# Two MLP matrices as seven block products in place of eight, in a two-layer streaming encoder step

## The chip, the core and the metric

The kernel runs on one core of one Trainium2 chip. The metric is the device time of one execution in microseconds (us), taken as the median of several runs. The engines are TensorE (PE in the profile; PEld is its weight load), VectorE (DVE), ScalarE (ACT), GpSimd (POOL) and SyncE (SP), which issues transfers.

## The reference

Two layers work on 1056 tokens (1024 of a prompt, 32 of a running sample) of width 1024. Layer 0 mixes tokens by forgetting attention, layer 1 by a gated linear recurrence; each is followed by a squared-ReLU MLP with a hidden width of 4096. Everything is float32.

```python
def rmsnorm(x, g):
    xf = x.astype(jnp.float32)
    y = xf * lax.rsqrt(jnp.mean(xf * xf, axis=-1, keepdims=True) + EPS)
    return (y * g.astype(jnp.float32)).astype(x.dtype)
...
        x = x + rmsnorm(out, post_mix_norm[layer])
        h = rmsnorm(x, pre_ffn_norm[layer])
        u = jax.nn.relu(h @ ffn_w_up[layer])
        x = x + rmsnorm((u * u) @ ffn_w_down[layer], post_ffn_norm[layer])
```

`out` is the mixer's output times W_out. The change rewrites the part from W_out to the last line, once per layer.

## The kernel before, in words

Activations lie with features on partitions and tokens along the free axis, in three chunks of C = 352 tokens. Every product is taken in float32r: a matrix is split exactly into a high and a low part, and `mm3` (L152) adds three passes, high by high, low by high, high by low, in one PSUM bank. A weight unit of 128 x 1024 comes in by DMA (`wr`); `load_w` (L122) casts the high part `wh` on ACT (L142) or POOL (L144), by turns, and DVE subtracts it to get the low part `wl` (L145).

`tail` (L436) is called once per layer. Its stages:

- Output projection (`po`), chunk by chunk, with all eight weight units loaded once. ACT copies each result out of PSUM, squares it, and POOL adds up the squares (L194). `postnorm` (L271) scales the chunk (L279, DVE) and adds the residual (POOL and DVE by turns, L162 and L284); `prenorm` (L222) splits the next product's input into `hh` and `hl` (ACT L226, DVE L231, POOL L162). The factor of the second norm, `prestat` (L236), is put on after the products, so the products don't wait for it.
- The MLP, two hidden tiles at a time. `up_one` (L491) takes 24 matmuls of 352 columns per hidden tile and chunk; ACT takes relu (L499) and the square's high part (L501), POOL squares again (L162), DVE subtracts (`ul`, L503). `down_one` (L510) takes, per two hidden tiles, 6 matmuls for each of eight output tiles and each chunk, and DVE adds the bank to the running sum `ya` (L520).
- The last two groups go chunk by chunk, so that `finish` (norms, and the next layer's input, or the output `y`) of one chunk lies beside the products of the next. In layer 1 the last chunk is normed with tokens on partitions (`end_open` L328, `end` L345).

One loop of the MLP holds 144 matmuls of `up` and 144 of `dn`; both layers together hold 4608 + 4608 of 352 columns.

The order in which an engine's instructions stand is set by the scheduler of the tile framework from the program's order; what stands in `with self.soon()` goes ahead of other work. Each engine works through its own list in order, so an instruction that waits holds back all behind it.

## Time and profile before

| | us |
|---|---|
| median of 3 runs | 3001.73 |
| lowest, highest | 2998.78, 3002.98 |
| profiled execution's span | 2996.0 |
| median less span | 5.7 |
| PE busy | 2942.2 (98%) |
| DVE busy | 1734.0 (58%) |
| ACT busy | 934.1 (31%) |
| POOL busy | 967.0 (32%) |
| mean granted TensorE clock | 0.997 of 2.4 GHz |

The span runs from the first to the last instruction; the median also holds what lies around it. PE's matmuls overlap in its pipeline, so the time of one is read from the distance between two starts, not from its own duration. Shares of busy time are means over stages: what holds a stage up is read from that stage's own window. Names such as `dn` and `ya` are the program's tiles, and L158 is a line of the kernel.

### The profile page before, as it was taken

The numbers are of one execution on the slowest core, as the hardware profiler recorded it, in microseconds if no ns is written. First come the engines' busy times: TensorE is split into PE (matmuls) and PEld (weight loads), VectorE is DVE, ScalarE is ACT, GpSimd is POOL, SyncE is SP. The second block draws the span as 40 slices with busy tenths as digits, with TensorE's granted clock in tenths as the row PEclk, the third lists the DMA queues.
The fourth block names the chain that finished last, engine by engine and source line by source line (L and its number), as shares of the span: only waits on it lengthen the run. The fifth ranks groups of instructions, "written<-read, shape, count | busy, mean of one in ns | idle before, by whom it ended". The sixth has DMA issues, their size and how long they took to land.

```text
span 2996.0 us, 46448 instructions
## 1 busy us (share of the span) xinstructions
PE 2942.2 (98%) x18511; PEld 2855.2 (95%) x18511; DVE 1734.0 (58%) x2980; ACT 934.1 (31%) x1915; POOL 967.0 (32%) x1151
## 2 busy tenths in 40 slices
...
GB/s 152 62 52 44 48 53 48 51 112 147 106 74 57 43 43 50 36 57 49 37 82 95 35 59 41 47 27 120 140 118 76 36 57 43 43 50 36 57 61 69
DMA packets 217817, 195.59 MB, mean 65 GB/s; under 512 B 14312, under 2 KB 193648, under 8 KB 217472
## 3 DMA queue, kind: packets, MB, share of 16 engines
q1 hardware_dynamic: 216576, 192.49, 21.5%
q8 instruction: 145, 2.38, 0.3%
...
q0 software_dynamic: 1024, 0.13, 0.0%
...
## 4 chain that ended last, share of the span: by engine, by line
PE 89%; DVE 5%; issue 1%; POOL 1%; ACT 1%; DMA 1%; SPq 0%; DVEq 0%; POOLq 0%; ACTq 0%
PE up L158 24%; PE dn L158 24%; PE hj L158 8%; PE pj L158 8%; PE gp L158 6%; PE po L158 5%; PE lv L1166 1%; PE ss L753 1%; PE pv L880 1%; PE pv L879 1%; PE pv L878 1%; PE st L867 1%; PE st L866 1%; PE mp L835 1%; PE lv L1181 1%
## 5 line engine op out<-in xcount | busy, mean ns | idle before, releaser
L520 DVE TENSOR_TENSOR ya<-dn,ya 128x352 f32<-128x352 f32 x672 | 348.3, 522 | 550.4 <-PE dn L158 550.4
L162 POOL TENSOR_TENSOR rl<-rl 128x352 f32<-128x352 f32 x192 | 190.2, 999 | 1031.7 <-ACT uh L501 1029.3
L145 DVE TENSOR_TENSOR wl<-wr,wh 128x1024 fp32r<-128x1024 f32 x203 | 280.4, 1382 | 147.0 <-ACT wh L142 84.6
L158 PE MATMUL dn<-uh,wl 128*128 128x352 f32 x1440 | 356.9, 323 | 0.0
L158 PE MATMUL dn<-uh,wh 128*128 128x352 f32 x1440 | 353.7, 324 | 2.5 <-DVE ya L520 2.5
L158 PE MATMUL dn<-ul,wh 128*128 128x352 f32 x1440 | 353.5, 323 | 0.0
L499 ACT ACTIVATE rl<-up 128x352 f32<-128x352 f32 x192 | 88.8, 463 | 783.1 <-PE up L158 712.8
L158 PE MATMUL up<-hh,wl 128*128 128x352 f32 x1536 | 291.5, 323 | 0.0
L158 PE MATMUL up<-hh,wh 128*128 128x352 f32 x1536 | 287.5, 323 | 2.1 <-ACT wh L142 1.7
L158 PE MATMUL up<-hl,wh 128*128 128x352 f32 x1536 | 288.1, 323 | 0.0
L158 PEld LDWEIGHTS up<-hh,wh 128*128 128x128 f32 x1536 | 253.5, 188 | 3.1 <-ACT wh L142 2.3
L158 PEld LDWEIGHTS dn<-uh,wh 128*128 128x128 f32 x1440 | 251.3, 188 | 4.4 <-DVE ya L520 4.4
L158 PEld LDWEIGHTS up<-hh,wl 128*128 128x128 f32 x1536 | 254.4, 188 | 0.0
L158 PEld LDWEIGHTS up<-hl,wh 128*128 128x128 f32 x1536 | 254.1, 188 | 0.0
L158 PEld LDWEIGHTS dn<-uh,wl 128*128 128x128 f32 x1440 | 252.6, 188 | 0.0
L158 PEld LDWEIGHTS dn<-ul,wh 128*128 128x128 f32 x1440 | 251.8, 188 | 0.0
L144 POOL TENSOR_SCALAR wh<-wr 128x1024 fp32r<-128x1024 f32 x109 | 120.8, 1108 | 294.3 <-PE pj L158 93.0
L503 DVE TENSOR_TENSOR ul<-rl,uh 128x352 fp32r<-128x352 f32 x192 | 142.6, 754 | 124.9 <-POOL rl L162 124.8
L142 ACT CAST wh<-wr 128x1024 fp32r<-128x1024 f32 x94 | 98.7, 1050 | 347.2 <-PE up L158 221.5
L876 DVE TENSOR_TENSOR pl<-pf,ph 128x512 fp32r<-128x512 f32 x192 | 124.5, 652 | 59.9 <-POOL ph L875 34.7
L875 POOL TENSOR_SCALAR ph<-pf 128x512 fp32r<-128x512 f32 x192 | 125.2, 654 | 51.6 <-PE pv L879 24.7
L869 ACT ACTIVATE pf<-st,ncol 128x512 f32<-128x512 f32 x192 | 109.7, 578 | 71.2 <-PE st L867 40.1
...
## 6 DMA issues: line engine op xcount, KB each, us to landing
wr<-in_ffn_w_up_dram SPq DMA_DIRECT2D x64, 512.0 KB, 4.0
wr<-in_ffn_w_down_dram SPq DMA_DIRECT2D x64, 512.0 KB, 3.8
wr<-in_fox_w_in_dram SPq DMA_DIRECT2D x32, 512.0 KB, 4.1
wr<-in_hgrn_w_in_dram SPq DMA_DIRECT2D x32, 512.0 KB, 4.1
...
```

Of the source, the lines that this page charges most:

```text
L142: self.s.copy(wh, raw)
L144: self.g.tensor_scalar(out=wh, in0=raw, scalar1=1.0, scalar2=0.0, op0=ALU.mult, op1=ALU.add)
L145: self.v.tensor_tensor(wl, raw, wh.bitcast(F32), op=ALU.subtract)
L158: self.nc.tensor.matmul(ps, lhsT=ws[kk][a], rhs=xs[kk][b], start=i == 0, stop=i == tot - 1)
L162: self.g.tensor_tensor(out, a, b, op=op)
L499: self.s.activation(rl, ps[:, :C], AF.Relu)
L503: self.v.tensor_tensor(ul, rl, uh.bitcast(F32), op=ALU.subtract)
L520: self.v.tensor_tensor(ys[n][:, o], ps[:, :C], ys[n][:, o], op=ALU.add)
L753: nc.tensor.matmul(ss[:, :C], lhsT=self.blk, rhs=sq, start=True, stop=True)
L869: self.s.activation(pf[:, :N], ps[:, :N], AF.Exp, bias=self.ncol[:, b, head:head + 1])
L875: self.g.tensor_scalar(out=ph[:, :N], in0=pf[:, :N], scalar1=1.0, scalar2=0.0, op0=ALU.mult, op1=ALU.add)
L876: self.v.tensor_tensor(pl[:, :N], pf[:, :N], ph[:, :N].bitcast(F32), op=ALU.subtract)
```

## The change

Tokens are taken in four quarters of G = 264; group c holds quarters c and c + 2, which play the two column blocks of the input. A unit is 256 rows by 256 columns of output by input features at a time, four pairs of feature tiles long: its four 128 x 128 blocks (`a11` to `a22`) and the two token quarters give seven products in place of eight, in the order 1, 5, 2, 6, 3, 7, 4 (`unit`). A product is 3 passes of 4 matmuls of 264 columns, so a unit has 84 matmuls per group and 168 for both.

- Weight side of a unit: 1 MB by DMA, four sums of blocks on POOL (`form`, 512 columns each), seven casts on ACT and seven subtracts on DVE (`cut`, 512 columns each), into a ring of three.
- Input side: seven forms of each pair of tiles, 7 x 264 columns, split in high and low (`forms`, `t_forms`, `split`).
- `up`: the results are put together by ACT copies, DVE adds from PSUM and a POOL add; relu and square are one DVE operation on each of four blocks; four POOL subtracts make the next product's forms, which go to memory (`uf`). The first NA = 4 units run for group 0 alone and again for group 1 alone, their weights loaded and formed twice; twelve run for both groups.
- `down`: step s takes the four pairs s - 3 to s for output block (s + 1) mod 4. `get_forms` brings a pair's forms back from memory and splits them. Steps 0 to 13 take both groups; 14 to 18 first group 0, then group 1, with group 0's `finish` ahead of group 1's step 15.
- The output projection goes by groups (`project`), with W_out loaded twice. The norm's factor is applied ahead of the product, as rows; the special form of the last chunk is gone. In the recurrence's projections ACT takes the results out of PSUM and no factor is multiplied on; chunks there are quarters.

In both layers together 10752 matmuls of 264 columns stand in place of 9216 of 352. The diff, cut to what is spoken of:

```diff
-TOK0 = (0, 128, C - 128)
+G = NT // 4
...
+LAG = 14
+NA = 4
+EV = 6
...
+    def forms(self, c, x, r, kind, layer, scratch, place):
+        for kp in range(4):
+            f = scratch(kp)
+            for j, o in ((2 * kp, f[:, 0:8:7]), (2 * kp + 1, f[:, 2:5:2])):
+                self.v.scalar_tensor_tensor(out=o, in0=x[:, j], scalar=self.gcol(kind, layer, j), in1=r,
+                                            op0=ALU.mult, op1=ALU.mult)
+            self.t_forms(f, (self.g, self.v, self.g, self.v))
+            self.F[c].append(place(kp))
+            self.split(self.F[c][kp], f[:, 0:7], 0, 7)
+    def t_forms(self, f, engs):
+        for e, o, a, b in zip(engs, (1, 5, 3, 6), (7, 4, 4, 2), (0, 7, 1, 3)):
+            e.tensor_tensor(f[:, o], f[:, a], f[:, b], op=ALU.subtract)
+    def split(self, F, src, a, b):
+        lo, hi = F[:, 0, a:b], F[:, 1, a:b]
+        self.s.copy(hi, src)
+        self.v.tensor_tensor(lo, src, hi.bitcast(F32), op=ALU.subtract)
+    def unit(self, cs, raw, pairs, evac):
+        nk = len(pairs)
+        w = raw.rearrange("p (k e) (m q) -> p k e m q", e=2, m=2)
...
+        def form(i, a, b=None, op=None):
+            self.ns += 1
+            t = self.S[:, self.ns % 3, :, 0:nk]
+            src = a
+            if b is not None:
+                self.nx += 1
+                src = self.Sx[:, self.nx % 2, 0:nk]
+                self.g.tensor_tensor(src, a, b, op=op)
+            S[i] = (t[:, 0], t[:, 1], src)
+        def cut(i):
+            lo, hi, src = S[i]
+            self.s.copy(hi, src)
+            self.v.tensor_tensor(lo, src, hi.bitcast(F32), op=ALU.subtract)
+        add, sub = ALU.add, ALU.subtract
+        ps = {}
+        for f, p in enumerate((1, 5, 2, 6, 3, 7, 4)):
+            if p == 1:
+                form(1, a11)
+            elif p == 5:
+                form(5, a21, a22, add)
+                form(2, a12)
+                form(6, S[5][2], a11, sub)
+            elif p == 6:
+                form(3, a12, S[6][2], sub)
+            elif p == 3:
+                form(7, a11, a21, sub)
+            elif p == 7:
+                form(4, a22)
+            cut(p)
+            lo, hi, _ = S[p]
+            fresh = p in (1, 5, 2, 4)
+            bank = {1: "X", 6: "X", 7: "X", 5: "Z", 3: "Z", 2: "Y", 4: "V"}[p]
+            for c in cs:
...
+                n, tot = 0, 3 * nk
+                for a, b in ((hi, 1), (lo, 1), (hi, 0)):
+                    for i, kp in enumerate(pairs):
+                        self.nc.tensor.matmul(o, lhsT=a[:, i], rhs=F[kp % 4][:, b, f], start=fresh and n == 0,
+                                              stop=n == tot - 1, skip_group_check=not fresh)
+                        n += 1
+                with self.soon():
+                    evac(p, c, o)
...
+    def tail(self, w_out, layer, sc=None):
...
+                def project(c):
+                    for o in range(NJ):
+                        wh, wl = self.load_w(self.col_unit(w_out, o * 128))
+                        for h in range(2):
...
+                        acc = self.sq_add(0, ys[c][:, o], o)
+                    return acc
+                acc = project(0)
+                acc2 = self.postnorm(0, ys[0], xa, acc, 1, layer, sc and sc(0))
+                self.put_x(0, xa)
+                scr = [ob.tile([128, 8, G], F32, name=f"fs{layer}_{i}") for i in range(2)]
+                self.forms(0, xa, self.factor(acc2), 2, layer, lambda kp: scr[kp % 2], lambda kp: form_tile(fa))
+                ys.append(pair(new(self.rh if last else ob, "yb", 16)))
+                acc = project(1)
+                xb = pair(new(self.rh, "xb", 16))
+                acc2 = self.postnorm(1, ys[1], xb, acc, 1, layer, sc and sc(1))
+                self.put_x(1, xb)
...
+            def up(i, cs, sts):
+                raw = load(wu[:, i * 256:i * 256 + 256].rearrange("(k p) m -> p k m", p=128))
...
+                def act(eng, c, slot, z):
+                    eng.scalar_tensor_tensor(out=st[c][:, slot], in0=z, scalar=0.0, in1=z, op0=ALU.max, op1=ALU.mult)
+                def evac(p, c, o):
...
+                        if p == 4:
+                            z = T[5, c]
+                            self.gtt(z, z, t, ALU.add)
+                            act(self.v, c, 4, z)
+                        self.v.tensor_tensor(t, o, t, op=ALU.add)
+                        act(self.v, c, {2: 0, 3: 7, 4: 2}[p], t)
+                    if p == 4:
+                        self.t_forms(st[c], (self.g, self.g, self.g, self.g))
+                        nc.sync.dma_start(self.uf[i][c], st[c][:, 0:7])
+                self.unit(cs, raw, range(4), evac)
+            for i in range(NA):
+                if i == 3:
+                    s = ust
+                else:
+                    s = fb.tile([128, 8, G], F32, name=f"us{layer}_{i}", tag=f"f{3 - i % 2}")
+                up(i, (0,), (s,))
+            with self.soon():
+                self.forms(1, xb, self.factor(acc2), 2, layer, lambda kp: fscr,
+                           lambda kp: form_tile(fb, tag=f"f{kp}"))
+            hst = [new(self.rh, "hs", 8) for i in range(4)]
+            for i in range(NA):
+                up(i, (1,), (hst[i % 4],))
+            for i in range(NA, 16):
+                up(i, (0, 1), (hst[2 * (i % 2)], hst[2 * (i % 2) + 1]))
+            Y = [pair(new(self.rh, "Y", 16)) for c in range(2)]
+            def get_forms(p, c, land):
+                for i, (a, b) in enumerate(((0, 2), (2, 4), (4, 6), (6, 7))):
+                    self.nl += 1
+                    t = land[:, 2 * (self.nl % 4):2 * (self.nl % 4) + b - a]
+                    nc.sync.dma_start(t, self.uf[p][c][:, a:b])
+                    self.split(self.F[c][p % 4], t, a, b)
+            def down(s, cs, load):
+                m = (s + 1) % 4
+                pairs = range(max(0, s - 3), min(s, 15) + 1)
+                first, final = s < 4, s > 14
+                r = pairs[0] * 256
+                raw = load(wd[r:r + 256 * len(pairs), m * 256:m * 256 + 256].rearrange("(k p) m -> p k m", p=128))
+                T = {}
...
+                def evac(p, c, o):
+                    y = lambda a, b: Y[c][:, 2 * m + a, b]
+                    if p in (5, 6, 7):
+                        t = T[p, c] = ev("e")
+                        self.s.copy(t, o)
+                    if p == 1 and first:
+                        self.s.copy(y(0, 0), o)
+                    elif p in (1, 2):
+                        self.v.tensor_tensor(y(0, 0), o, y(0, 0), op=ALU.add)
+                    elif p == 7:
+                        w = T[5, c]
+                        if not first:
+                            self.gtt(w, w, y(1, 1), ALU.add)
+                        self.gtt(y(1, 1), w, t, ALU.add)
+                    elif p in (3, 4):
+                        t, d = (T[6, c], y(0, 1)) if p == 3 else (T[7, c], y(1, 0))
+                        if not first:
+                            self.gtt(t, t, d, ALU.add)
+                        self.v.tensor_tensor(d, o, t, op=ALU.add)
+                        squares(c, 0 if p == 3 else 1)
+                self.unit(cs, raw, pairs, evac)
+            self.acc, self.nsq, self.nl = [None, None], [0, 0], 0
+            for s in range(LAG):
+                for c in range(2):
+                    get_forms(s, c, st)
+                down(s, (0, 1), load)
+            get_forms(LAG, 1, st)
+            for s in range(LAG, 19):
+                if s < 16:
+                    get_forms(s, 0, st)
+                down(s, (0,), load)
...
+            def finish(c):
+                acc = self.postnorm(c, Y[c], xs[c], self.acc[c], 3, layer, more=not last)
...
+                for j in range(NJ):
+                    y = xs[c][:, j]
+                    self.v.scalar_tensor_tensor(out=y, in0=y, scalar=self.gcol(0, layer + 1, j), in1=r,
+                                                op0=ALU.mult, op1=ALU.mult)
+                    self.s.copy(hh[:, j], y)
+                    (self.g if j % 3 == 2 else self.v).tensor_tensor(hl[:, j], y, hh[:, j].bitcast(F32), op=ALU.subtract)
+            self.h = [None, None]
+            for s in range(LAG, 19):
+                if s == 15:
+                    finish(0)
+                    get_forms(s, 1, st)
+                down(s, (1,), load if s < 15 else load2)
+            finish(1)
```

How the order moves, at three places. DVE at the start of layer 0's MLP: `rw` is the norm's factor per token, `yo`, `x` and `hl` the last chunk's norm and split, `ul` the MLP's own subtract. Before:

```order
L279 SCALAR_TENSOR_TENSOR yo_9250<-yo_9250,gain,rw_9497 128x352 x8
L503 TENSOR_TENSOR ul_9622<-rl_9682,uh_9621 128x352
L284 TENSOR_TENSOR x_0_9482<-x_0_9482,yo_9250 128x352 x2
L284 TENSOR_TENSOR x_1_9483<-x_1_9483,yo_9250 128x352
L231 SCALAR_TENSOR_TENSOR hl_9548<-x_0_9482,gain,hh_9547 128x352
L284 TENSOR_TENSOR x_1_9483<-x_1_9483,yo_9250 128x352
L231 SCALAR_TENSOR_TENSOR hl_9548<-x_1_9483,gain,hh_9547 128x352
L231 SCALAR_TENSOR_TENSOR hl_9548<-x_0_9482,gain,hh_9547 128x352
L241 TENSOR_TENSOR yo_9250<-yo_9250 128x352
L231 SCALAR_TENSOR_TENSOR hl_9548<-x_0_9482,gain,hh_9547 128x352
L503 TENSOR_TENSOR ul_9624<-rl_9712,uh_9623 128x352
```

and now, where `fs` is the scratch of group 1's input forms, `F` their split, `Y`/`e`/`hs` the evacuation of group 1's first unit and `S` the cuts of weights:

```order
L260 SCALAR_TENSOR_TENSOR fs_938_10034<-xb_932_9976,gain,rr_10555 128x2x264 x2
L270 TENSOR_TENSOR fs_938_10034<-fs_938_10034 128x264 x2
L276 TENSOR_TENSOR F_981_10596<-fs_938_10034,F_981_10596 128x1848
L260 SCALAR_TENSOR_TENSOR fs_938_10034<-xb_932_9976,gain,rr_10555 128x2x264 x2
L270 TENSOR_TENSOR fs_938_10034<-fs_938_10034 128x264 x2
L276 TENSOR_TENSOR F_982_10605<-fs_938_10034,F_982_10605 128x1848
L530 TENSOR_TENSOR e_10628<-Y_10651,e_10628 128x264
L518 SCALAR_TENSOR_TENSOR hs_983_10608<-e_10628 128x264
L301 TENSOR_TENSOR S_10038<-Sx_10039,S_10038 128x512 x2
```

Before, subtracts of the running product stand between the pieces of the norm. Now the forms of group 1 stand in one block, of which the last rows are shown (the same three kinds come four times), behind the last unit of group 0 and ahead of group 1's first.

DVE at the end of layer 0: the norm of a finished chunk or group. Before, with `dn` the products of the next chunk:

```order
L279 SCALAR_TENSOR_TENSOR ya_9898<-ya_9898,gain,rw_15960 128x352 x8
L284 TENSOR_TENSOR x_0_15942<-x_0_15942,ya_9898 128x352 x2
L520 TENSOR_TENSOR ya_9899<-dn_16067,ya_9899 128x352
L284 TENSOR_TENSOR x_1_15943<-x_1_15943,ya_9898 128x352
L231 SCALAR_TENSOR_TENSOR hl_16015<-x_0_15942,gain,hh_16014 128x352
L284 TENSOR_TENSOR x_1_15943<-x_1_15943,ya_9898 128x352
L520 TENSOR_TENSOR ya_9899<-dn_16084,ya_9899 128x352
L231 SCALAR_TENSOR_TENSOR hl_16015<-x_0_15942,gain,hh_16014 128x352
L520 TENSOR_TENSOR ya_9899<-dn_16101,ya_9899 128x352
L241 TENSOR_TENSOR ya_9898<-ya_9898 128x352
L231 SCALAR_TENSOR_TENSOR hl_16015<-x_1_15943,gain,hh_16014 128x352
```

and now, `Y_1211` being group 0's sum, `xs` the residual, `Y_1212` group 1's sum and `S` the cuts of weights of group 1's step 15:

```order
L241 SCALAR_TENSOR_TENSOR Y_1211_13968<-Y_1211_13968,gain,rr_17809 128x528 x8
L243 TENSOR_TENSOR xs_1444_17682<-xs_1444_17682,Y_1211_13968 128x528 x4
L232 TENSOR_TENSOR st_8900<-st_8900 128x528 x2
L276 TENSOR_TENSOR F_982_10605<-st_8900,F_982_10605 128x528 x2
...
L634 SCALAR_TENSOR_TENSOR xs_1444_17682<-xs_1444_17682,gain,rr_17859 128x528 x8
L585 TENSOR_TENSOR Y_1212_13969<-X_17917,Y_1212_13969 128x264
L301 TENSOR_TENSOR S_10038<-Sx_10039,S_10038 128x512
L637 TENSOR_TENSOR h_1466_17877<-xs_1444_17682,h_1465_17876 128x528
L301 TENSOR_TENSOR S_10038<-Sx_10039,S_10038 128x512
```

Before, the adds that empty PSUM stand between the norm's rows from the third on. Now the scaling, the adds and the next layer's scaling of group 0 stand ahead of the first cut of group 1's step.

POOL in the steady part of the first product. Before, squares of `rl` and casts of weights:

```order
L144 TENSOR_SCALAR wh_11808<-wr_11806 128x1024
L162 TENSOR_TENSOR rl_11597<-rl_11597 128x352
L162 TENSOR_TENSOR rl_11847<-rl_11847 128x352
L162 TENSOR_TENSOR rl_11877<-rl_11877 128x352
L144 TENSOR_SCALAR wh_12196<-wr_12194 128x1024
L162 TENSOR_TENSOR rl_11907<-rl_11907 128x352
```

and now, where `Sx` are sums of weight blocks, `hs` the forms of the result and `e` evacuated products:

```order
L295 TENSOR_TENSOR Sx_10039<-raw_940_10036 128x512
L295 TENSOR_TENSOR Sx_10039<-raw_941_10037 128x512
L295 TENSOR_TENSOR Sx_10039<-Sx_10039,raw_941_10037 128x512
L270 TENSOR_TENSOR hs_985_10610<-hs_985_10610 128x264
L270 TENSOR_TENSOR hs_986_10611<-hs_986_10611 128x264
L186 TENSOR_TENSOR e_12833<-e_12833,e_12958 128x264
L270 TENSOR_TENSOR hs_985_10610<-hs_985_10610 128x264 x2
L186 TENSOR_TENSOR e_12848<-e_12848,e_12972 128x264
L295 TENSOR_TENSOR Sx_10039<-raw_941_10037,Sx_10039 128x512
```

Before, one operation of 352 columns per 24 matmuls and a cast now and then. Now sums of 512 and of 264 columns follow one another, all of them two tensors from SBUF.

## Rows read from the trace of the kernel before

**Rows 1.** The page's span, and part 1: busy time of each engine.

```profile
span 2996.0 us, 46448 instructions
PE 2942.2 (98%) x18511; PEld 2855.2 (95%) x18511; DVE 1734.0 (58%) x2980; ACT 934.1 (31%) x1915; POOL 967.0 (32%) x1151
```

**Rows 2.** Part 4 of the page: the chain's share by line.

```profile
PE up L158 24%; PE dn L158 24%; PE hj L158 8%; PE pj L158 8%; PE gp L158 6%; PE po L158 5%; PE lv L1166 1%; PE ss L753 1%; PE pv L880 1%; PE pv L879 1%; PE pv L878 1%; PE st L867 1%; PE st L866 1%; PE mp L835 1%; PE lv L1181 1%
```

**Rows 3.** The chain in order of time (start us, us, what), MLP of layer 0.

```profile
956.07 7.76 PE up L158 x48
1002.46 7.76 PE up L158 x48
```

**Rows 4.** Windows: length, busy us (x count) per engine, PE clock, DMA share, GB/s.

```profile
728.00:917.50 189.50, 186.93 (x1173) 185.15 (x1172) 90.79 (x130) 78.45 (x171) 75.43 (x73) 1.00 0.31 102
917.50:1493.50 576.00, 576.00 (x3579) 576.00 (x3579) 267.47 (x423) 92.39 (x171) 101.63 (x98) 1.00 0.16 46
1493.50:1640.00 146.50, 131.28 (x795) 126.85 (x795) 103.55 (x170) 55.85 (x118) 74.22 (x77) 0.97 0.28 88
```

**Rows 5.** Timeline of PE at 167 us: start us, us, operation, columns.

```profile
167.44 0.28 PE L866 MATMUL st<-QA,KA 128*128 128x256 f32 x1
167.55 0.28 PE L867 MATMUL st<-QX,KB 97*128 97x256 f32 x1
167.68 0.32 PE L158 MATMUL pj<-hl,wh 128*128 128x352 f32 x1
...
168.40 0.23 PE L866 MATMUL st<-QA,KA 128*128 128x128 f32 x1
168.46 0.28 PE L867 MATMUL st<-QX,KB 97*128 97x128 f32 x1
```

**Rows 6.** Three lines' instructions: ns min/median/max, first and last start.

```profile
L503 DVE TENSOR_TENSOR ul<-rl,uh x192: 506/525/1409, 823.8 to 2944.1; 128x352 fp32r<-128x352 f32 x192
L520 DVE TENSOR_TENSOR ya<-dn,ya x672: 507/524/527, 910.7 to 2982.6; 128x352 f32<-128x352 f32 x168
L194 POOL TENSOR_TENSOR sa<-sa,sj x72: 928/947/1807, 730.8 to 2981.3; 128x352 f32<-128x352 f32 x72
```

**Rows 7.** Timelines of DVE, then of POOL, at 2214 us.

```profile
2214.40 1.26 DVE L241 TENSOR_TENSOR yo<-yo 128x352 f32<-128x352 f32 x1
2215.59 3.64 DVE L231 SCALAR_TENSOR_TENSOR hl<-x,gain,hh 128x352 fp32r<-128x352 f32 x3
...
2214.08 1.20 POOL L194 TENSOR_TENSOR sa<-sa,sj 128x352 f32<-128x352 f32 x1
2215.25 1.22 POOL L162 TENSOR_TENSOR hl<-yo,hh 128x352 fp32r<-128x352 f32 x1
2216.43 1.23 POOL L241 TENSOR_TENSOR yo<-yo 128x352 f32<-128x352 f32 x1
2217.62 1.22 POOL L194 TENSOR_TENSOR sa<-sa,sj 128x352 f32<-128x352 f32 x1
```

**Rows 8.** Parts 5 (busy us, mean ns) and 6 (KB, us to landing) of the page.

```profile
L144 POOL TENSOR_SCALAR wh<-wr 128x1024 fp32r<-128x1024 f32 x109 | 120.8, 1108 | 294.3 <-PE pj L158 93.0
L142 ACT CAST wh<-wr 128x1024 fp32r<-128x1024 f32 x94 | 98.7, 1050 | 347.2 <-PE up L158 221.5
wr<-in_ffn_w_up_dram SPq DMA_DIRECT2D x64, 512.0 KB, 4.0
```

**Rows 9.** Timeline of PE: the last two matmuls of `dn`.

```profile
2981.91 0.48 PE L158 MATMUL dn<-ul,hh 128*128 128x352 f32 x2
```

**Rows 10.** Timeline of PE behind a stop at 1581 us.

```profile
1586.49 4.24 PE L158 MATMUL hj<-hh,wh 128*128 128x352 f32 x16 [4.91 <-ACT sj L191]
1590.57 1.46 PE L158 MATMUL hj<-hh,wl 128*128 128x352 f32 x8
```

587 lines of the change are left out of this document (225 added, 362 removed).

## The prediction

> **What bounds the kernel now.** I read the page's engine shares first: TensorE (PE) is busy 98% of a span of 2996.0 us, VectorE (DVE) 58%, ScalarE (ACT) 31%, GpSimd (POOL) 32% [rows 1]. The chain that ended last says the same by line: `up` and `dn`, the two MLP products, hold 24% each [rows 2]. In order of time the chain shows the MLP's beat: a run of 48 `up` matmuls begins every 46.39 us [rows 3]. Two hidden tiles by three chunks of 24 matmuls, and eight output tiles by three chunks of 6, are 288 matmuls, so one of 352 columns takes 46.39 / 288 = 0.161 us. The windows show what fills the beat: in 576.0 us PE is never idle, while DVE works 267 us and POOL 102 [rows 4]. Around the MLP it is otherwise: between 1493.5 and 1640 us, where one layer's last norms run into the next projection, PE is busy 131 of 146.5 us [rows 4]. So the MLP is bound by matmuls, and its edges by elementwise work. The change must be weighed at both.
>
> **What it removes.** Per layer 16 + 16 units of 168 matmuls of 264 columns replace 4608 of 352. In both layers 9216 become 10752. A matmul's time follows its columns: neighbours of 256 start 0.11 to 0.13 us apart, one of 128 is followed after 0.06, 352 need 0.161 [rows 3, 5]. I take 264 / 352 of 0.161 = 0.1208 us (0.116 would be the low end from 256 columns, 0.1214 the high one from a line through 128 and 352). 9216 x 0.161 = 1484 and 10752 x 0.1208 = 1299 us: **186 us less**, an eighth (179 to 237 by the ends). A unit for both groups then lasts 168 x 0.1208 = 20.3 us, for one group 10.1.
>
> **What it adds: two engines that must take turns.** Block sums, splits and forms are elementwise with both inputs in SBUF. What such work costs beside POOL is in the trace. DVE's `ul` subtract (two SBUF inputs) takes 525 ns in the middle and up to 1409; its `ya` add on the same 352 columns, with one input from PSUM, never leaves 507 to 527; POOL's `sa` add takes 947 and up to 1807 [rows 6]. The stretch at 2214 us shows why: DVE and POOL step together, POOL starting every 1.18 us where it needs 0.947 alone, each DVE operation stretched to 1.2 [rows 6, 7]. A pair of 352 columns costs both engines 1.19 us. I split this as 525 to 947: 1.21 ns a column for DVE's two-SBUF work, 2.17 for POOL's, to be added where both are loaded. DVE's PSUM operations and ACT stay out of the sum. The Trainium skill, "SBUF — State Buffer", section "SBUF: two separate sides", calls the shared port pair an exclusive lock for the whole instruction. By that, full durations would add, 1.47 us a pair; the row has 1.19, so the measurement is used and the rule becomes a rival below.
>
> *Per unit.* The weight side is four POOL sums and seven DVE subtracts of 512 columns (seven ACT casts of 512 beside them, at 1050 ns for 1024 [rows 8] at most 7.4 us, hidden). Up, per group: four DVE activations, and five POOL sums of 264. Down, per group: 1848 columns of DVE split and four POOL sums of 264.
> - Up, both groups: 5696 x 1.21 + 4688 x 2.17 = 17.1 us of taking turns, under 20.3 of PE: hidden.
> - Down, both: 7280 x 1.21 + 4160 x 2.17 = 17.8: hidden, with 2.5 us to spare.
> - Up, one group: 4640 x 1.21 + 3368 x 2.17 = 12.9, **over** 10.1 of PE. The weight side doesn't shrink when one group uses it.
>
> *Norm and forms of one group.* DVE: scaling 8 x 528, adds 4 x 528, squares 2 x 528, gains 16 x 264, forms 8 x 264, splits 4 x 1848, factors 8 x 264: 23232 columns. POOL: adds 4 x 528, squares 5 x 528, forms 8 x 264: 6864. 28.1 + 14.9 = 43 us. Before, the like of it for a chunk lay beside other chunks' products: from 728 to 917.5 us PE was idle only 2.6 us [rows 4].
>
> **Where this lands on the path,** place by place, the work that takes turns against PE's:
> - Out projection of group 1 (384 matmuls, 46.4 us) beside group 0's norm and forms: 43, plus eight `wl` subtracts of 1024 (9.9), four POOL casts at 1108 ns [rows 8] (4.4) and squares (7.0) = 64. Loss 18 a layer.
> - The four units for group 0 alone (40.6) beside group 1's norm and forms. In DVE's order the forms stand behind the last unit's cuts and ahead of group 1's first; so PE waits for them: 4 x 12.9 + 43 = 95, loss 54.
> - The same four units again for group 1: 51.6 against 40.6, loss 11.
> - Steps 14 to 18 for group 0 alone: the pairs run out (4, 4, 3, 2, 1), so 294 matmuls, 35.5 us. DVE: 3.5 x 3584 of cuts, two pairs' splits, squares: 17296 columns; POOL: 3.5 x 2048 of sums, 20 x 264, squares: 15088. 53.7, loss 18.
> - The same for group 1, with group 0's finish in DVE's and POOL's queues ahead of step 15's cuts: in layer 0 14784 and 5808 columns more (30.5), in layer 1, without squares, forms and splits, 6336 and 2112 (12.2). 84 and 66 against 35.5: loss 49 and 30.
> - Group 1's finish: in layer 0 30.5 against 144 matmuls of the next projection that group 0 allows (17.4), loss 13; in layer 1 nothing is left, loss about 21.
>
> Twice 18 + 54 + 11 + 18 is 202, and 49 + 30 + 13 + 21 is 113: 315 us. Given back are the old stalls: 3 and 18 us (146.5 less 795 x 0.161) [rows 4] and 14 behind the last `dn` at 2982 [rows 9], together 35. 315 - 35 - 186 = **+94 us**.
>
> **Edits with one answer.** The inner forms go to memory and back, 1.9 MB a unit, written in one stage and read in the other, beside 1 MB of weights: 2.9 MB in 20.3 us, some 140 GB/s in a stage that now moves 46 at a DMA share of 0.16 [rows 4], so half the queues' time, and a whole step ahead; nothing. W_out loaded twice: its DMA lands in 4 us like other weights [rows 8], the casts are counted. The hgrn evacuation on ACT and 264-column chunks move the same columns; nothing, within 10 us either way. Restarts: after 4.91 us of idle, 16 matmuls took 4.1 us for 2.6 [rows 10], so 1.5 us a stop and under 20 for all places; I leave it in the range, since stalls made of many short waits need not cost it. The Trainium skill, "TensorE: Matmul & The Clock Gate", section "Back-to-back issue gap", has columns / 2.4 + 2.5 ns for an isolated matmul; by that 264 would take 112.5 and the sum fall by 89 us, to +5. For 352 it gives 149 where the beat has 161, so it is not used.
>
> The sum is against the profiled execution: 2996.0 + 5.7 around the span is the median of 3001.7. Forecast: **3096 us**, slower by 3.1%.
>
> **Rivals.**
> - *The two engines rarely meet* (faster). Where POOL's and DVE's operations fall into each other's gaps, or wait for ACT anyway, each place costs only its busier engine at undisturbed durations, 1.49 ns a DVE column and 2.69 of POOL. Then the out projection costs nothing (46), group 0's four units 67 - 41 = 26, group 1's nothing, group 0's ends 5 (POOL 40.6 against 35.5), group 1's 21 and 11, the finishes 5 and 18. 2 x (26 + 5) + 55 = 117; 117 - 35 - 186 = -104, **2898 us**. For it: most `ul` subtracts are undisturbed [rows 6]. Against: these are the places where both queues are full, as at 2214 us [rows 7]. It decides if the pair costs less than about 0.9 us.
> - *The steady units slip too* (much slower). 17.1 to 17.8 of 20.3 us leaves 12 to 16%, with in-order queues, three buffers for cut weights (two products, 5.8 us, ahead) and two for sums. If each of the 52 two-group units slips by 1.5 us, 78 more: **3174 us**. For it: DVE carries PSUM adds on top, six to eight a unit. Against: before, DVE had the same sort of mixture at 46% and PE never waited [rows 4].
> - *The lock holds for the whole instruction.* With 1.49 and 2.69 ns added, up takes 21.1 and down 22.0 us per unit, so 34 us a layer are lost in the steady part alone; group 0's four units lose 76, the projection 32, group 1's units 23, the ends 31, then 68 and 46, 20 and 25: 551 in all, 330 over before, **3332 us**. Against it: rows 7 beside rows 6, 1.19 and not 1.47. By the Trainium skill's rule that is quoted above from "SBUF — State Buffer" it would go so.
> - *Matmuls of 264 don't get shorter in proportion.* At 0.1214, +6 us; part of the range.
>
> **How the numbers follow.** Forecast 0.47, with 3040 to 3150 of its own; engines rarely meet 0.25; steady units slip 0.18; whole-instruction lock 0.07; what I don't see 0.03. No change means within 0.2%, 6 us, about what a measurement of this kernel can tell. The first rival is all below that, the others above; the unseen is shared out: faster 0.26, same 0.02, slower 0.72. The range, 2885 to 3210, leaves out the whole-instruction lock and the outer third of the fast case.
>
> **What would show it.** In the changed profile: `Y`, `X`, `Z`, `V` matmuls 0.121 us apart and a two-group unit in 20.3 us with PE busy throughout; PE with holes, and a granted clock below full after them, in the four-unit stages, the single-group steps and around the finishes, DVE and POOL full there; the split subtracts of 528 stretched well over 0.78 us where POOL works. The forecast is wrong if PE stays full in the four-unit stage (then the engines do not take turns there), or if the two-group units last 21.5 us or more.

## The result and the profile after

The changed kernel takes **3227.8 us** (median of 4, 3224.5 to 3229.4) against 3001.1 for the kernel before: ratio 1.0756, 95% interval 1.0741 to 1.0771, **7.6% slower**. The sign was as forecast, the size was not: +227 us where the sum gave +94, and outside the range of 2885 to 3210.

The page after; span and busy time of each engine [rows 1], then the chain's shares [rows 2]:

```profile
span 3226.6 us, 55945 instructions
PE 2885.5 (89%) x21197; PEld 2747.2 (85%) x21197; DVE 2287.1 (71%) x3589; ACT 1374.5 (43%) x2904; POOL 1747.8 (54%) x1801
PE 70%; DVE 15%; issue 5%; POOL 3%; ACT 3%; DMA 3%; SPq 0%; DVEq 0%; POOLq 0%; ACTq 0%
```

PE was busy 98% and is now busy 89%; DVE holds 15% of the chain. In order of time, the chain in the steady part of layer 0's first product is the counterpart of [rows 3]: the seven products of a two-group unit, 24 matmuls each, and the first of the next unit.

```profile
1010.19 2.92 PE X L333 x24
1013.10 2.95 PE Z L333 x24
1016.05 2.91 PE Y L333 x24
1018.96 2.94 PE X L333 x24
1021.90 2.92 PE Z L333 x24
1024.82 2.93 PE X L333 x24
1027.76 2.92 PE V L333 x24
1030.68 2.91 PE X L333 x24
```

A unit lasts 1030.68 - 1010.19 = 20.49 us, 0.122 us a matmul where the sum had 0.1208: the product side was right within 1%. The windows of after, in the columns of [rows 4], show where the time went. In order: four units of group 0; group 1's first unit; its other three; the twelve two-group units; steps 0 to 2 of the second product; steps 3 to 13; steps 14 to 18 of group 0; the same of group 1; the start of the next layer's projection; then, of layer 1, the four units of group 0, the last steps of group 1 and the tail.

```profile
850.60:936.20 85.60, 55.31 (x341) 51.27 (x341) 77.11 (x91) 30.05 (x59) 64.31 (x49) 0.78 0.40 130
936.20:971.60 35.40, 15.26 (x88) 13.49 (x87) 22.34 (x25) 9.73 (x13) 11.71 (x11) 0.64 0.00 0
971.60:1010.40 38.80, 35.02 (x254) 32.94 (x254) 35.89 (x44) 16.33 (x34) 32.77 (x27) 0.96 0.48 162
1010.40:1256.40 246.00, 246.00 (x2019) 246.00 (x2018) 168.12 (x258) 87.31 (x189) 173.45 (x168) 1.00 0.40 145
1256.40:1303.90 47.50, 37.78 (x254) 34.56 (x253) 39.91 (x70) 27.64 (x70) 22.33 (x25) 0.86 0.69 219
1303.90:1528.90 225.00, 225.00 (x1850) 225.00 (x1850) 170.55 (x247) 106.99 (x231) 140.35 (x124) 1.00 0.47 142
1528.90:1580.00 51.10, 43.44 (x295) 38.81 (x294) 43.98 (x61) 25.62 (x60) 41.33 (x42) 0.96 0.43 139
1580.00:1676.40 96.40, 53.52 (x302) 46.23 (x300) 78.55 (x104) 40.54 (x87) 66.55 (x58) 0.77 0.26 80
1676.40:1760.00 83.60, 44.61 (x314) 42.69 (x315) 49.36 (x56) 28.10 (x53) 35.48 (x32) 0.74 0.22 67
2363.80:2467.80 104.00, 60.06 (x345) 53.70 (x345) 97.67 (x114) 37.22 (x70) 71.76 (x54) 0.73 0.35 118
3109.30:3191.60 82.30, 59.00 (x346) 49.02 (x344) 63.11 (x88) 32.57 (x73) 56.09 (x51) 0.83 0.23 75
3191.60:3226.60 35.00, 11.91 (x52) 7.43 (x52) 19.98 (x26) 6.18 (x12) 8.68 (x7) 0.60 0.19 62
```

PE is never idle in the fourth and sixth rows (DVE is busy 68 and 76% there, POOL 71 and 62%); everywhere else it has holes, and in the first row DVE is busy 77 of 85.6 us. So the rival in which the steady units slip did not happen, nor the one in which a whole instruction locks the other engine out. The Trainium skill, "SBUF — State Buffer", section "SBUF: two separate sides", has the shared port pair as an exclusive lock for the whole instruction. By that rule the rival put a two-group unit at 21.1 to 22.0 us, and the chain above has 20.49. The margin is smaller than it looks: with the undisturbed durations of `e10` below (DVE 692 ns for 512 columns, 708 for 528, 434 for 264) and those of POOL's sums beside an idle DVE in the changed kernel (1288 ns for 512, 750 for 264), the rival's sum is about 21 us for both kinds of unit, by my estimate.

The elementwise groups that replace those of [rows 6], from part 5 of the page:

```profile
L301 DVE TENSOR_TENSOR S<-Sx,S 128x512 fp32r<-128x512 f32 (+3 forms) x352 | 305.1, 871 | 105.8 <-ACT S L300 105.0
L295 POOL TENSOR_TENSOR Sx<-raw 128x512 f32<-128x512 f32 (+3 forms) x176 | 234.6, 1335 | 167.4 <-DVE S L301 162.9
L270 POOL TENSOR_TENSOR hs<-hs 128x264 f32<-128x264 f32 x224 | 221.6, 1004 | 93.0 <-DVE hs L518 91.3
```

Two holes have names of their own. PE's timeline (start, length, line; in brackets the idle time before and what ended it) in layer 0, in group 1's step 15 and at the start of the next layer's projection:

```profile
1623.46 2.13 PE L205 MATMUL cs<-st,ones 128*128 128x264 f32 x4 [25.14 <-DVE st L232]
...
1713.00 2.13 PE L205 MATMUL cs<-st,ones 128*128 128x264 f32 x4 [25.71 <-DVE st L232]
1726.76 3.54 PE L182 MATMUL hj<-h,wh 128*128 128x264 f32 x16 [11.64 <-ACT wh L166]
```

`cs` are a norm's squares, summed over partitions by a matmul with ones. They stand in PE's list ahead of products that don't depend on them, and wait for the squares that `finish` sums up late. DVE's timeline in the first of these holes:

```profile
1603.42 8.64 DVE L241 SCALAR_TENSOR_TENSOR Y<-Y,gain,rr 128x528 f32<-128x528 f32 x8
1611.99 5.86 DVE L243 TENSOR_TENSOR xs<-xs,Y 128x528 f32<-128x528 f32 x4
1617.77 0.69 DVE L232 TENSOR_TENSOR st<-st 128x528 f32<-128x528 f32 x1
1622.70 0.71 DVE L232 TENSOR_TENSOR st<-st 128x528 f32<-128x528 f32 x1 [4.24 <-POOL st L232]
```

**Place by place.** The table compares the two traces between the same matmuls. A loss is a place's length less the matmuls of its product, at 0.161 us before and 0.1208 after; the columns hold the loss after less the loss before, in us, over both layers, rounded. The last column is an experiment that is told below (`e10`: no sums on GpSimd in the tail). The "rival" is the prediction's first, in which the two engines rarely meet.

| Place | forecast | rival | measured | e10 |
|---|---|---|---|---|
| ahead of the output projection | 0 | 0 | 11 | 8 |
| output projection, to the MLP's start | 33 | -3 | 31 | 14 |
| first four units, group 0 then 1 | 130 | 52 | 175 | 82 |
| two-group units and steps 3 to 13 | 0 | 0 | 9 | 8 |
| steps 0 to 2 | 0 | 0 | 34 | 27 |
| steps 14 to 18, group 0 | 36 | 10 | 30 | 11 |
| steps 14 to 18, group 1 | 79 | 32 | 108 | 56 |
| inside the MLP of before | 0 | 0 | -38 | -38 |
| next projection and recurrence | -5 | -13 | 35 | 18 |
| tail | 7 | 4 | 21 | 16 |
| sum | 280 | 82 | 415 | 203 |
| matmuls | -186 | -186 | -185 | -185 |

415 - 185 = 230 is the difference of the spans (3226.6 - 2996.0; the rows are rounded). 280 - 186 is the forecast's +94. The row of matmuls is no measurement: it takes the prediction's two prices. At the beats that the chains show, 0.1611 and 0.1220 us, the products save 173 us, and the 12 us between stand as losses, 9 of them in the row of the two-group units. Of the 38 us "inside the MLP of before" only some 8 are waits; the rest are other matmuls that ran there, 48 of them (7.7 us) of the next projection, so without these that row is -30 and the projection's 27.

### The profile page after: what moved, and what is told of

The parts are those of the page before. It is cut to its first block, busy times and chain, and to the rows that moved or that the text cites. A ratio compares the mean times of both kernels' runs of the same rounds, so it can differ in the third digit from the quotient of the medians.

```text
span 3226.6 us, 55945 instructions
## 1 busy us (share of the span) xinstructions
PE 2885.5 (89%) x21197; PEld 2747.2 (85%) x21197; DVE 2287.1 (71%) x3589; ACT 1374.5 (43%) x2904; POOL 1747.8 (54%) x1801
## 4 chain that ended last, share of the span: by engine, by line
PE 70%; DVE 15%; issue 5%; POOL 3%; ACT 3%; DMA 3%; SPq 0%; DVEq 0%; POOLq 0%; ACTq 0%
PE X L333 14%; PE Z L333 9%; PE hj L182 9%; PE pj L182 7%; PE Y L333 5%; PE gp L182 5%; PE V L333 4%; DVE S L301 3%; PE po L182 3%; DVE F L276 2%; PE lv L1218 1%; DMA st<-uf 1%; PE pv L934 1%; PE pv L932 1%; PE pv L933 1%
## 5 line engine op out<-in xcount | busy, mean ns | idle before, releaser
L333 PE MATMUL X<-F,S 128*128 128x264 f32 x4608 | 654.7, 294 | 125.3 <-ACT F L275 65.5
L333 PEld LDWEIGHTS X<-F,S 128*128 128x128 f32 x4608 | 605.3, 194 | 149.9 <-ACT F L275 69.2
L333 PE MATMUL Z<-F,S 128*128 128x264 f32 x3072 | 437.6, 294 | 39.6 <-DVE S L301 27.8
L333 PEld LDWEIGHTS Z<-F,S 128*128 128x128 f32 x3072 | 406.8, 195 | 52.7 <-DVE S L301 36.0
L301 DVE TENSOR_TENSOR S<-Sx,S 128x512 fp32r<-128x512 f32 (+3 forms) x352 | 305.1, 871 | 105.8 <-ACT S L300 105.0
L295 POOL TENSOR_TENSOR Sx<-raw 128x512 f32<-128x512 f32 (+3 forms) x176 | 234.6, 1335 | 167.4 <-DVE S L301 162.9
L301 DVE TENSOR_TENSOR S<-raw,S 128x512 fp32r<-128x512 f32 (+3 forms) x264 | 248.9, 946 | 66.5 <-ACT S L300 66.1
L276 DVE TENSOR_TENSOR F<-st,F 128x528 fp32r<-128x528 f32 (+1 forms) x256 | 224.3, 881 | 77.8 <-ACT F L275 77.5
L182 PE MATMUL pj<-H,wh 128*128 128x352 f32 x1152 | 254.2, 338 | 0.6 <-POOL wh L162 0.5
L182 PE MATMUL hj<-h,wh 128*128 128x264 f32 x1536 | 225.4, 291 | 13.3 <-ACT wh L166 13.1
```

The lines of the kernel that those rows point to most:

```text
L182: self.nc.tensor.matmul(ps, lhsT=ws[kk][a], rhs=xs[kk][b], start=i == 0, stop=i == tot - 1)
L276: self.v.tensor_tensor(lo, src, hi.bitcast(F32), op=ALU.subtract)
L295: self.g.tensor_tensor(src, a, b, op=op)
L301: self.v.tensor_tensor(lo, src, hi.bitcast(F32), op=ALU.subtract)
L333: self.nc.tensor.matmul(o, lhsT=a[:, i], rhs=F[kp % 4][:, b, f], start=fresh and n == 0, stop=n == tot - 1, skip_group_check=not fresh)
```

## The experiments

Two theories were put against each other. **A**: DVE's work with two inputs in SBUF and POOL's work take turns, so the edges cost the sum of both. **B**: chains, that is operations that wait for each other one by one, and in-order queues. All times are medians; the ratio is to the kernel before, with its 95% interval. Stage lengths are read from the traces as in the table.

**e1: DVE reads one tensor.** The two-input operations in the tail read one.

```diff
-        self.v.tensor_tensor(lo, src, hi.bitcast(F32), op=ALU.subtract)
+        self.one_v(lo, hi.bitcast(F32))
+    def one_v(self, out, a):
+        return self.v.tensor_scalar(out=out, in0=a, scalar1=1.0, scalar2=0.0, op0=ALU.mult, op1=ALU.add)
...
```

> From the output projection to the end of each layer's MLP, every VectorE operation that reads two tensors from SBUF now reads one (the low part is a copy of the high part, products and sums keep one factor or term; the first of each row of eight keeps both), with the same shape, count and order of waits; GpSimd's work is unchanged. So the norms, splits, forms and activations are only partly computed. Theory A (the edges are set by VectorE and GpSimd taking turns at SBUF): the stretched VectorE operations fall to their undisturbed length (512 columns from 871 to about 690 ns), GpSimd's too (264-column differences from 1004 to about 630 ns), the four units of one group take 45 to 70 us instead of 86 and 104, and the time falls from 3228 to between 3030 and 3110. Theory B (the edges are chains in which each operation waits for one on another engine, in queues served in order): shorter links alone, 3150 to 3200. Theory C (VectorE's own operations fill the edges): their count stays, so 3200 to 3228.

Measured: 3102.2 us, 1.034 [1.0323, 1.0357], 126 less, in theory A's range. The four units of group 0 fell from 85.6 to 59.9 us in layer 0. But the instructions of one kind (shortest / median / longest ns) show that two things changed at once:

```profile
L296 DVE TENSOR_SCALAR F<-F x272: 280/487/2162, 794.8 to 3024.0; 128x528 fp32r<-128x528 f32 x119, 128x264 fp32r<-128x264 f32 x9, 128x1848 fp32r<-128x1848 f32 x8
L296 DVE TENSOR_SCALAR st<-st x28: 416/435/1524, 757.5 to 3079.4; 128x528 f32<-128x528 f32 x28
```

An operation of 528 columns with one input takes 435 ns undisturbed, with two about 708 (e10, below), and it is still stretched, to 1524 ns. So e1 shows that this work is on the path, and not whether by its amount or by turns.

**e3 and e9: fewer single-group units.** `NA` is 2, then 0; e9 also has the edit of e2.

```diff
-NA = 4
+NA = 2
```

> NA = 2: two units instead of four run for group 0 alone and again for group 1 alone; fourteen run for both groups. Theory A: a unit alone takes 12.9 us of turns, twice 25.8, a unit for both groups 20.5: 2 units x 2 layers x 5.3 us = 21 us less, 3207. Theory B: group 1's norm and forms are a chain that takes its time whatever lies beside it, so the two units' matmuls leave a cover that costs nothing now and are done in the open: 3228 to 3250.

> NA = 0 with two scratches: no unit runs for one group alone; group 1's norm and forms have no products beside them, and all sixteen units run for both groups. Theory A: from NA = 2 (3207) another 21 us less by units, and 13 by the scratches: 3173. Theory B: the two units' products (20 us a layer) lose their place beside the chain: 3200 to 3230.

Measured: 3207.0 us, 1.0693 [1.0677, 1.0709], and 3171.7, 1.0578 [1.056, 1.0595]. Theory A had said 3207 and 3173. Forming the weights twice for two groups costs what the columns of both engines cost. The rows say it directly: where nothing but weights and results lies beside the products, in group 1's other three units, a unit takes 38.8 / 3 = 12.9 us (12.6 in layer 1), the sum's figure, and in e10 below, without POOL's sums, 10.2, its matmuls alone.

**e10: no sums on GpSimd in the tail.** Copies on ACT, or nothing, stand in; POOL only casts weights.

```diff
-                self.g.tensor_tensor(src, a, b, op=op)
+                src = a
...
-            e.tensor_tensor(f[:, o], f[:, a], f[:, b], op=ALU.subtract)
+            if e is self.g:
+                self.s.copy(f[:, o], f[:, a])
...
```

> From the output projection to the end of each MLP, GpSimd does nothing but casts of weights: its block sums are left out, and its differences, adds and squares are copies or squares on ScalarE; VectorE's operations keep both inputs. So sums, forms, residuals and norms are only partly computed. If the two engines' turns are the one cost that my sum got right, this is like the run with one input, 3102, give or take 15. If GpSimd's operations also count as links of a chain (0.6 to 1.75 us each, where a copy on ScalarE takes 0.4 to 0.65), it is clearly below that: 3030 to 3085. If VectorE's undisturbed work alone filled the edges, it stays above: 3110 to 3130.

Measured: 3015.5 us, 1.0051 [1.0036, 1.0066], 212 less and below all three ranges. Its page, and its windows of group 0's four units, group 1's first unit, steps 0 to 2 and the last steps of group 1:

```profile
PE 2813.5 (93%) x21197; PEld 2708.9 (90%) x21197; DVE 1903.1 (63%) x3589; ACT 1535.9 (51%) x3304; POOL 534.8 (18%) x735
```

```profile
837.40:894.30 56.90, 46.72 (x342) 45.60 (x342) 45.45 (x86) 37.84 (x81) 0.00 (x0) 0.89 0.58 199
894.30:925.60 31.30, 14.77 (x88) 13.42 (x88) 20.48 (x27) 13.34 (x22) 0.00 (x0) 0.63 0.02 4
1202.30:1246.50 44.20, 35.46 (x254) 33.76 (x254) 29.47 (x66) 28.52 (x76) 0.00 (x0) 0.88 0.73 242
1513.20:1583.20 70.00, 47.25 (x302) 44.37 (x301) 50.08 (x100) 42.48 (x95) 0.98 (x1) 0.75 0.33 104
```

DVE runs the same 3589 instructions in 1903.1 us where it needed 2287.1: 384 us of its busy time came from POOL's work beside it. But even alone it leaves PE idle: 203 us of losses stay (table), where the rival had 82. The 203 are not exactly what the changed kernel would lose without turns, since ACT's copies are new work (ACT is busy 1535.9 us for 1374.5) and some sums have no stand-in.

**e16: GpSimd beside, but nobody waits for it.** e10, and POOL does a sum of the same size again beside each stand-in, into a scratch.

```diff
+    def beside(self, a, b):
+        d = self.dm[:, 0:2] if len(a.shape) == 3 else self.dm[:, 0]
+        self.g.tensor_tensor(d, a, b, op=ALU.add)
...
                 self.s.copy(f[:, o], f[:, a])
+                self.beside(f[:, a], f[:, b])
```

> The kernel of e10, in which copies on ACT stand in for GpSimd's sums in the tail (so sums of blocks, of forms, of squares and of the residual are left out there), and beside each of them GpSimd does a sum of the same size again: it reads the same tiles, or one of them twice, and writes a scratch that nobody reads. So GpSimd has the work of the changed kernel (3227.8 us) and takes its turns with DVE, but nobody waits for its results; only buffers wait for its reads. e10 without that work was 3015.5. If the turns alone set the edges (theory A), the time comes back to 3150 to 3230 us and the first four units of layer 0 to 75 to 90 us. If waits for GpSimd's results do (theory B: slow links in a chain), it stays at 3015 to 3070 and the four units at 57 to 65. In between, what lies above 3015.5 is the turns' part and what lies below 3227.8 the links' part; e1 had suggested some 125 and 87 us, which would be 3140, but it had also shortened DVE's own operations.

Measured: 3205.1 us, 1.0684 [1.0666, 1.0702]: 190 of the 212 us come back. The page and two windows (group 0's four units, steps 3 to 13):

```profile
PE 2866.8 (89%) x21197; PEld 2731.6 (85%) x21197; DVE 2339.8 (73%) x3589; ACT 1509.5 (47%) x3304; POOL 1731.2 (54%) x1801
```

```profile
842.10:930.30 88.20, 51.51 (x341) 48.00 (x341) 82.10 (x91) 38.69 (x81) 67.33 (x51) 0.81 0.37 127
1297.90:1533.90 236.00, 232.47 (x1850) 227.00 (x1849) 178.69 (x246) 112.15 (x252) 139.28 (x122) 1.00 0.44 134
```

The four units are back at 88.2 us (85.6 in the changed kernel, 56.9 in e10), though no cast or cut waits for a sum. Steps 3 to 13, which the changed kernel does in 225, take 236.0 and, in layer 1, 240.9 us here, 27 that the changed kernel doesn't have (probably buffers that wait for POOL's reads; nothing separates this); without these the turns make 163. So of the 212 us, 163 to 190 are turns. What is left, 22 to 49 us, fits waits for POOL's results, which no run isolates.

**e2: two scratches for group 1's forms.** In the changed kernel each pair of tiles goes through one scratch.

```diff
-                self.forms(1, xb, self.factor(acc2), 2, layer, lambda kp: fscr,
+                self.forms(1, xb, self.factor(acc2), 2, layer, lambda kp: (fscr, st)[kp % 2],
```

> Group 1's input forms are made in two scratch tiles by turns (the second is the tile of squares, which is free then) instead of one. Now the first unit of group 1 waits 12 us for the first pair and 6.7 us for each of three more. Theory A: the same columns take the same turns, so the pairs still come 5 to 7 us apart: 3220 to 3228. Theory B: a pair's chain VectorE, GpSimd and VectorE, ScalarE, VectorE is what takes 7.3 us, and two of them overlap: 6 to 12 us less in each layer, 3204 to 3216.

Measured: 3214.1 us, 1.0711 [1.0695, 1.0727], in theory B's range; group 1's first unit 26.4 and 27.0 us in place of 35.4 and 35.8. DVE's timeline of the changed kernel shows one link of that chain:

```profile
937.92 1.45 DVE L260 SCALAR_TENSOR_TENSOR fs<-xb,gain,rr 128x528 f32<-128x528 f32 x2
939.40 0.85 DVE L270 TENSOR_TENSOR fs<-fs 128x264 f32<-128x264 f32 x1
940.89 0.43 DVE L270 TENSOR_TENSOR fs<-fs 128x264 f32<-128x264 f32 x1 [0.64 <-POOL fs L270]
943.12 2.08 DVE L276 TENSOR_TENSOR F<-fs,F 128x1848 fp32r<-128x1848 f32 x1 [1.80 <-ACT F L275]
945.24 1.45 DVE L260 SCALAR_TENSOR_TENSOR fs<-xb,gain,rr 128x528 f32<-128x528 f32 x2
```

Scale, form, cast (ACT), subtract, and only then the next pair: 945.24 - 937.92 = 7.3 us, of which DVE works 4.8 (2.1 of it the subtract). In e10, without POOL, pairs still come 6.3 us apart, of which DVE works 4.4 and waits 1.8 for ACT's cast. The sum had costed this chain by its columns alone.

**e4, e5 and e15: the holes around `finish`.** e4 moves group 0's next scaling and split in layer 0 behind group 1's last step. e5 takes the factor of the next layer's first norm from older sums. e15 adds to e5 that each weight serves group 0's quarters first and that POOL casts and subtracts the third weight.

```diff
-                r = self.factor(acc)
+                r = self.factor(self.acc[c])
...
-            for n in (0, 2, 1, 3):
+            for ns in ((0, 2), (1, 3)):
...
```

> In layer 0 the second half of group 0's finish (scaling, casts and subtracts for the next layer, 7392 columns on VectorE and 1056 on GpSimd, 11 us of turns) stands behind group 1's last step, not ahead of its step 15. Theory A: the same turns, moved to where nothing but group 1's finish runs: 3222 to 3234. Theory B: step 15's cuts come 10 to 18 us earlier, and the moved part falls in the waits of group 1's finish: 3208 to 3220.

> At the end of layer 0 the factor of the next layer's first norm is taken from the sums of squares that the factor before it used, which are ready early; the sums of the new squares are still made and added up, and nobody reads them. So that norm's factor is not the reference's. Theory A: the same columns on both engines, 3222 to 3228. Theory B: PE's own sums of squares stand in its queue ahead of products that are ready, 25.5 us at 1624 and 26 us at 1713; without that wait 96 products of the next projection (11.7 us) come ahead and the scaling starts without the squares: 15 to 35 us less, 3193 to 3213.

> The changed kernel with the early sum of e5 (the next layer's first norm uses the sums of squares from before the last group), and two more edits in the next layer's first projection: each of the first three weights is used for the quarters of group 0 and then of group 1 (quarters in pairs 0,2 and 1,3 as one block of the program), and the third weight is cast and subtracted on POOL, so that it doesn't stand behind group 1's casts on ACT or subtracts on DVE. e5 alone was 3222.5 us, with holes of 28.7 us (a cut of a weight) and 33.4 us (the third weight's cast) left. If the place of the third weight in ACT's and DVE's queues makes the second hole (theory B, in-order queues), more of group 0's 144 matmuls run ahead of group 1's and the time falls by 12 to 20 us below e5: 3202 to 3210. If the amount of DVE's and POOL's work between the last product and group 1's input sets the stretch (theory A), the hole moves once more and the time stays at 3218 to 3226.

Measured: e4 3226.1 us, 1.0755 [1.0739, 1.0771], the last steps 96.5 as before; e5 3222.5, 1.0742 [1.0726, 1.0758], both as theory A had it; e15 3213.0, 1.0709 [1.0693, 1.0725], between its two ranges. The second hole in PE's timeline, in e5 and then in e15:

```profile
1721.50 3.89 PE L182 MATMUL hj<-h,wh 128*128 128x264 f32 x16 [32.78 <-ACT wh L166]
```

```profile
1710.92 2.10 PE L182 MATMUL hj<-h,wh 128*128 128x264 f32 x8 [31.15 <-ACT f L1134]
```

With the sums out of the way PE waits as long for the third weight's cast, and with that on POOL as long for ACT to empty a bank: each stands in an in-order queue behind group 1's norm. ACT's timeline in e15 shows it for the bank, a copy that comes right behind the norm's casts:

```profile
1708.51 1.99 ACT L636 CAST h<-xs 128x528 fp32r<-128x528 f32 x3 [2.00 <-DVE xs L634]
1710.40 0.65 ACT L1134 COPY f<-hj 128x264 f32<-128x264 f32 x2
```

The two edits of e15 together took 9.5 us off e5; which of them did is not separated. The hole itself is about as long as group 1's `finish` keeps DVE at work (in e5 from 1690 to 1723 us). No run has the `cs` matmuls themselves behind group 0's products.

**e6 and e14: steps 0 to 2.** e6 leaves out the transfer of the forms from memory. e14 leaves out the splits of the first three pairs.

```diff
-                    self.split(self.F[c][p % 4], t, a, b)
+                    if p > 2:
+                        self.split(self.F[c][p % 4], t, a, b)
```

> The inner forms are not brought back from memory: each split of the second product reads what stands in the landing tile, so the second product is of other data; stores to memory, casts and subtracts stay. Steps 0 to 2 of the second product now lose 17 us in each layer (18, 14 and 16 us for 5, 10 and 15 us of products). If the transfers and their ring of four landing pieces set that, 10 to 14 us come back in each layer: 3200 to 3208. If the casts and subtracts for two groups set it (4592 and 5488 columns on VectorE at 1.49 ns are 6.8 and 8.2 us a step), it stays within 5 us a layer: 3218 to 3228.

> The changed kernel, with one thing left out: in the second product the splits (cast on ACT, subtract on DVE) of the forms of the first three pairs of tiles, for both groups and both layers, so those products use what the buffers held before. Steps 0 to 2 lasted 50 us where their matmuls need 30.5, so 34 us are lost in both layers together; my sum set these at nothing. If the splits' columns on DVE, taken in turns with POOL's sums, set these steps (theory A), 3 x 2 x 1848 columns x 1.21 ns = 13.4 us less work of DVE per layer and the same from ACT: steps 0 to 2 fall to 36 to 42 us in each layer and the kernel to 3204 to 3212 us. If the links of one product set them (a sum on POOL, its cast, its cut, and the copy out of PSUM, one after another for short products; theory B), the steps stay at 46 to 51 us and the kernel at 3220 to 3228.

Measured: e6 3234.5 us, 1.0782 [1.0766, 1.0798], steps 0 to 2 in 50.0 and 50.7 us, so 7 us longer in all, above both its ranges and unexplained; e14 3219.2, 1.073 [1.0712, 1.0748], 44.0 and 43.0 where the changed kernel has 47.6 and 47.0, between its two ranges. The window of e14 in layer 0:

```profile
1253.90:1297.90 44.00, 35.86 (x255) 34.22 (x254) 23.61 (x46) 17.70 (x48) 20.89 (x25) 0.84 0.35 122
```

DVE is busy 23.6 of 44.0 us, ACT and POOL less, and PE still needs 13.5 us more than its matmuls. With one, two or three pairs a product has 6, 12 or 18 matmuls for both groups, 0.7 to 2.2 us, and each needs a sum, a cast and a cut, one after another, and a bank emptied. The transfers do not set these steps, and the splitting accounts for 8 of the 34 us lost there. That the rest is the links of one product is what is left, and no run shows it by itself.

**e8: more matmuls, higher clock.** Where PE has holes its granted clock is 0.60 to 0.96 (windows above). e8 puts six matmuls whose result nobody reads behind each single-group product.

> In the units of one group six matmuls of 264 columns into a bank that nobody reads stand behind each product (0.72 us at full clock; 126 products a layer). Nothing else changes. In these stages the trace shows 56 us of matmuls that follow one another at 0.22 us in place of 0.12, with a granted clock of 0.73 to 0.83. If the halved clock is on the path, the fillers keep it up and 15 to 45 us come back: 3183 to 3213. If VectorE and GpSimd set the pace (theory A) and the slow matmuls lie beside them, nothing comes back, and where a product is ready the fillers delay it: 3228 to 3260.

Measured: 3281.9 us, 1.0942 [1.0926, 1.0958], 54 more, above both its ranges. Windows of group 1's other three units and of group 0's last steps:

```profile
975.50:1020.90 45.40, 45.40 (x374) 45.40 (x374) 30.09 (x44) 16.91 (x32) 30.98 (x28) 1.00 0.35 123
1538.70:1601.50 62.80, 62.10 (x500) 61.20 (x499) 38.33 (x62) 28.22 (x62) 40.11 (x44) 1.00 0.36 116
```

The clock is full, PE has hardly a hole, and both stages are longer (45.4 for 38.8, 62.8 for 51.1): PE now has half as many matmuls again, which nobody needs, so these two don't say what the low clock costs. In layer 0, group 0's four units and group 1's last steps say more: PE still has holes there, the granted clock goes from 0.78 and 0.77 to 0.88, and they last 88.9 and 97.5 us for 85.6 and 96.4. A higher clock brought no shorter stage there either, though the fillers' own cost is in it. What the low clock costs in the changed kernel stays open. At most it is some 37 us on the units' matmuls that follow one another: 375 of them, at a granted clock of 0.5 (1.2 GHz), stand 0.22 us apart for 0.12 (208, or 21 us, in e10), and an unknown part of these lies beside other waits.

**e11 to e13: both groups together.** `NA` is 0, `LAG` 19, with e2's scratches: no single-group steps, one more pair of slots for the squares. e12 adds up the norms' squares on PE in place of POOL; e13 does that for one norm and gives the norms' and forms' other sums on POOL to DVE.

```diff
-LAG = 14
-NA = 4
+LAG = 19
+NA = 0
...
-            self.t_forms(f, (self.g, self.v, self.g, self.v))
+            self.t_forms(f, (self.v, self.v, self.v, self.v))
```

> NA = 0, two scratches, and LAG = 19: the last five steps of the second product are for both groups too, and both groups are finished behind them. The same arithmetic. Theory A: five steps for each group alone are twice 53.7 us of turns, together 71 us of products that cover them; group 0's finish, now in the open, was in the sum already. So 36 us less a layer than with NA = 0 (3172): 3100. Theory B (the cover of products is lost to two finishes one behind the other): 3160 to 3200.

> As the run before, and the sums of squares of the out projection and of the norms that feed another norm are made by PE, which adds eight tiles up in two banks, in place of seven adds on GpSimd and VectorE each (2640 and 1056 columns, 7.0 us of turns). The same arithmetic in another order. Theory A: two such sums are in the open in each layer's front and two in layer 0's finish: 6 x 7 = 42 us less than the run before, about 3058; if a part is hidden under the out projection, 20 to 42. Theory B (the chain waits as long for PE): within 10 us of the run before.

> From the run with the groups together (3108): in the norms behind the out projection and behind the MLP, in the forms of the first product and in layer 0's last splits VectorE does what GpSimd did (2112 + 2112 columns of a group's norm and forms, 2112 + 1056 of a finish), and the squares of the norms that feed another norm are added up by PE. The same arithmetic in another order; the block sums of weights, the squares of the out projection and the MLP's own sums stay on GpSimd. By the turns alone (1.21 in place of 2.17 ns a column, and 7.0 us of squares) 4 + 7 us go in each front and 3 + 7 in each of layer 0's two finishes, 45 us in all: about 3063. If GpSimd's operations also are the slow links of these chains, 60 to 90 us go: 3020 to 3048. If PE's sums and VectorE's longer queue take the place: within 15 us of 3108.

Measured: e11 3107.9 us, 1.0361 [1.0346, 1.0377]; e12 3106.4, 1.0356 [1.0339, 1.0374]; e13 3080.8, 1.0268 [1.0254, 1.0282]. Theory A had said 3100 for e11. For e12 it had said 20 to 42 us less than e11, and 1.5 came: the first unit's loss fell from 51 to 41 us and from 70 to 55, but the output projection ahead of it grew by as much. e13 is 27 us under e11, where turns alone gave 45, and in none of its three ranges. It is the best form of the seven products that was found, and still 2.7% over eight.

## Why the prediction was right in sign and wrong in size

**Right.** The beat: 20.49 us a unit for 20.3, by which the products save 173 us for 186. The steady units are hidden. The transfers from memory are hidden (e6 took nothing off). The mechanism at the edges: turns between DVE and POOL, 12.9 us for a single-group unit as forecast. And the price of the turns. Forecast less rival was 198 us (280 - 82 in the table), which is what meeting POOL was thought to add; POOL's sums in fact cost 212 (e10), 163 to 190 of it as turns (e16). By place it holds less well, with misses both ways: first units 93 measured for 78, group 1's last steps 52 for 47, output projection 17 for 36, group 0's last steps 19 for 26; so that the totals meet within 14 us is in part luck. The amounts that e3, e9, e11 and e4 move cost what their columns say, within 8 us; those of e12 and e13 do not.

**Wrong: the floor under it.** The step that failed is "place by place, the work that takes turns against PE's": it costs a place by the amount of its engines' work, columns by a price each, as if every cast, link and wait lay beside that. The rival used the same step with no turns, and gave 82 us of net losses; with POOL out of the way the chip shows 203. So, taking e10 for the kernel without turns, 121 of the 135 us that were missed (415 - 280) are there without any, and 14 in the turns. Their main places:
- *Norm and forms of group 1* were "43 us of work"; the forms are four links through one scratch, 7.3 us each, and a second scratch took 14 us off (e2).
- *Steps 0 to 2* have no term in the sum, and no reason for that: 34 us, 27 without POOL. The splits are 8 of the 34 (e14), the transfers nothing (e6); the rest is put down to the links of short products, which is argued and not tested.
- *The finishes.* The sum hid group 1's finish behind the 144 matmuls that group 0 allows (loss 13, with 18 given back). PE ran only 48 of them before its own `cs`, and then waited 25.7 and 11.6 us. The product of group 0 was there, but in-order queues on PE, ACT and DVE each hold something of group 1 ahead of it (e5, e15). In group 1's last steps it is a hole of the same kind, 25.1 us.
- *The tail*: 35.0 us where the sum had 21, without a working (13.9 before [rows 9]).

Against this stand the 38 us inside the MLP of before, mostly other matmuls, of which the 35 us that the sum gave back held some 4; without them the miss would have been larger still. What the 11 us ahead of the output projection are, no run shows. One price of the rival needs a word too: its 67 us for group 0's four units come out only with DVE's adds from PSUM, which the forecast leaves out (62 without).

**The range.** Restarts at a low clock were left in it at under 20 us; that they are so small is not shown (at most some 37 us between the units' matmuls, see e8). Its upper end came from rivals on the steady part, which kept its beat; that the edges' own sum could be short had no rival of its own, though every place was costed by the same step.
